# Router products inside the output projection, a float32 scatter, one more ring tile and a token-major last MLP

## The chip, the cores and the metric

The kernel runs on one core of a Trainium2 chip. The metric is the device time of one execution in microseconds (us). TensorE (PE) does the matrix products, and its weight loads (PEld) overlap them; VectorE (DVE) and ScalarE (ACT) do the elementwise work; GpSimd (POOL) is nearly idle; SyncE (SP) issues the DMA transfers that bring the weights from memory.

## The reference

Two blocks run one after the other on one sequence of 256 tokens of width 1024, each with two layers, all in float32.

```
def first_block(...):                       # two layers
        mod = c_act @ w_ada[layer] + b_ada[layer]        # 6 vectors: shifts, scales, gates
        h = rmsnorm(x, norm_mix_g[layer]) * (1.0 + sc_mix) + sh_mix
        mixed = token_mixer(h, ...)                      # SSD + HGRN + retention, then @ w_out
        x = x + g_mix * mixed
        h = rmsnorm(x, norm_ffn_g[layer]) * (1.0 + sc_ffn) + sh_ffn
        moe = hierarchical_moe(h, ...)                   # 32 experts in 4 groups, top 2, width 256
        x = x + g_ffn * moe
...
def second_block(...):                      # two layers, mixers RG-LRU and gated linear attention
        x = x + gt_m * rmsnorm_2(y, norm_g[i, 1])
        h = rmsnorm_2(x, norm_g[i, 2]) * (1.0 + sc_f) + sh_f
        y = conv_ffn(h, ...)                             # (gelu(conv(up)) * conv(up)) @ w_down
        x = x + gt_f * rmsnorm_2(y, norm_g[i, 3])
```

## The kernel before

**Layout.** Activations lie with channels on the partitions: `self.x` is 128 partitions x 8 channel groups x 256 tokens. A dense product is taken in three float32r matmuls (`mm3`, L517): both factors are split into a high part (rounded to float32r, `wh` by ACT in L509) and a rest (`wl` by DVE in L510), and the product of the two rests is dropped. Products that are written in plain float32 appear in the trace as two matmul instructions each.

**Weights.** Every weight comes as a tile of 1 MB by a DMA on SP's queue, in one fixed list (`make_plan`), into a ring of tiles (`Ring`): 8 tiles from the start, 3 more (`NM`) to the end of the mixture of experts, 6 more (`NX`) from the output projection on, and `NY` more from the start of the mixture of experts on. A transfer is issued when a tile of the ring comes free (`done`, `pump`), so SP stands still while the ring is full.

**The modulation vectors** (`ada`, tile `ad`, L299) are products of the conditioning vector with 96 weight tiles; four matmuls (eight instructions) a tile. Tables of numbers (`PRE`, `MIX`, `MOE`, `SP`, `FILL`) say how many of these tiles are taken up at which place in the list of weights and in TensorE's program.

**A layer of the first block.** After the token mixer, `out_proj` makes four projections `t` of 48 matmuls (tile `pj`), each for channel groups `2t` and `2t+1`; DVE adds each to `x`. `then(k)` makes the router's products for channel group `k`: two transposes (`htp`, L891), two products with the router's weights and two sums of squares (`rsum`, L893 and L896). They follow one projection later, and those of groups 6 and 7 at the end. Then come four `ad` tiles (`SP[7]`), while DVE works out the routing in a chain of small operations that ends in the one-hot matrix `oh`; `rkp` (L970) ranks the tokens of each expert.

**The mixture of experts** (`moe`) handles the 32 experts in eight blocks of four with 32 slots for each expert, and one further block `x` for a fully loaded expert, in the order 0 to 6, `x`, 7. For each block: `gp` (L1055) gathers the tokens of the slots, `gu` (L1095) makes gate and up products, `hdt` turns them, `dn` (L1136) makes the down product, and `scatter` (tile `ya`, L1153) adds the slots to the tokens through a matrix `P` of zeros and ones. For the scatter, the result `dn` is kept as a float32r high part `ys0` (a copy by ACT, L1140) and a rest `ys1` (a subtraction by DVE, L1141), and each of the eight channel groups takes two matmuls. Scatter of block `b` stands behind `gu` of block `b+2`. `overflow` (L1195) is a branch that would redo experts with more tokens than slots; here it is not taken.

**The second block.** Each of its two layers ends in `ffn`: 22 up products (`fup`, two projections of 128 channels each, with convolution and gelu) give `F`, and 22 x 8 x 3 = 528 matmuls (tile `fd`) multiply `w_down` (stationary) with `F` (256 tokens moving). After the last layer, `residual` scales and normalises the result and adds it to `x`, and four DMAs write `x` out.

## Time and profile before

| | |
|---|---|
| median of 3 runs | 1569.04 us (1565.69 to 1571.34) |
| the profiled execution | 1566.22 us, of which the span in the trace is 1564.1 us |
| granted TensorE clock, mean | 0.966 of full speed |
| busy: PE, DVE, ACT, POOL | 93%, 53%, 42%, 0% of the span |
| moved by DMA | 453.02 MB, 290 GB/s on average |

The share of busy time is an average over stages. In the two mixtures of experts (about 220 to 444 us and 645 to 870 us) the DMA engines are full; in the two MLPs of the second block TensorE is. What a piece of work costs is therefore to be read stage by stage, from what each stage waits for last.

### The profile page before, as it was taken

To read this page: it belongs to the slowest core of one execution; us is meant where nothing else is said; L and a number is where in the kernel's file an instruction comes from. 1 tells how busy PE (TensorE), PEld (TensorE's weight loads), DVE (VectorE), ACT (ScalarE), POOL (GpSimd) and SP (SyncE) were. 2 spreads that over 40 slices of the span, in tenths; PEclk is the share of its full clock that TensorE was granted. 3 is DMA by queue.
4 is the path that set the end of the run, shared out by engine and by line. 5 is a ranking of instruction groups with operands and counts; after the bars stand their busy time and mean duration, and the time that the engine had idled before them with its cause. 6 is when DMAs were issued, how large, how long until landed. Compare 5 with 4: busy or idle time off the path is not lost. (4 is left out here: it accounts for less than half of the span.)

```text
span 1564.1 us, 28414 instructions
## 1 busy us (share of the span) xinstructions
PE 1447.1 (93%) x11988; PEld 1143.9 (73%) x11988; DVE 824.1 (53%) x1580; ACT 656.1 (42%) x1098; POOL 3.0 (0%) x11
## 2 busy tenths in 40 slices
PE   4999999878989999897889999999999999899997
PEld 2868876434457778754445688799996997799996
DVE  3585631100157755311011667888846675788853
ACT  3534522111144254321121486566634544466643
POOL 0000000000000000000000000000000000000000
PEclk8999999989989999999899999999999999999999
DMA  9976789999998368899999877955546644655520
GB/s 379 420 278 243 277 326 421 421 421 420 416 393 348 121 243 329 333 420 420 421 420 415 335 291 283 375 190 186 176 159 245 244 162 157 221 193 185 189 82 28
DMA packets 64954, 453.02 MB, mean 290 GB/s; under 512 B 7088, under 2 KB 7728, under 8 KB 11440
## 3 DMA queue, kind: packets, MB, share of 16 engines
q1 hardware_dynamic: 63520, 446.94, 73.5%
q10 hardware_dynamic: 1296, 4.15, 0.7%
q8 instruction: 98, 1.61, 0.4%
q14 instruction: 40, 0.33, 0.1%
HBM read 450.01 MB, written 1.05 MB: 288 GB/s over the span
## 5 line engine op out<-in xcount | busy, mean ns | idle before, releaser
L517 PE MATMUL pj<-act,wh 128*128 128x256 f32 x3136 | 582.1, 287 | 20.3 <-ACT act L464 12.6
L517 PEld LDWEIGHTS pj<-act,wh 128*128 128x128 f32 x3136 | 494.8, 194 | 55.9 <-ACT act L464 15.3
L517 PE MATMUL pj<-act,wl 128*128 128x256 f32 x1568 | 446.2, 285 | 0.6 <-DVE wl L510 0.6
L510 DVE TENSOR_TENSOR wl<-wt,wh 128x1024 fp32r<-128x1024 f32 x260 | 317.2, 1223 | 222.7 <-ACT wh L509 220.0
L509 ACT ACTIVATE wh<-wt 128x1024 fp32r<-128x1024 f32 x260 | 274.3, 1059 | 345.8 <-PE pj L517 269.4
L517 PEld LDWEIGHTS pj<-act,wl 128*128 128x128 f32 x1568 | 303.3, 193 | 3.0 <-issue 1.2
L1095 PE MATMUL gu<-wt,xsl 128*32 128x256 f32 x2048 | 148.5, 410 | 36.8 <-DMA wt<-in_wu 33.8
L1095 PEld LDWEIGHTS gu<-wt,xsl 128*32 128x32 f32 x2048 | 72.4, 117 | 103.2 <-DMA wt<-in_wu 44.9
L517 PE MATMUL fd<-F,wh 128*128 128x256 f32 x704 | 125.0, 281 | 0.0
L1136 PE MATMUL dn<-wt,hT 128*32 128x512 f32 x528 | 114.5, 613 | 0.9 <-ACT hT L1116 0.9
L299 PE MATMUL ad<-wt,cz 128*32 128x512 f32 x768 | 112.9, 614 | 0.0
L517 PEld LDWEIGHTS fd<-F,wh 128*128 128x128 f32 x704 | 107.8, 188 | 0.2 <-ACT wh L509 0.2
L1104 DVE SCALAR_TENSOR_TENSOR sg<-sg,inf,gu 128x256 f32<-128x256 f32 x16 | 7.7, 480 | 180.6 <-ACT sg L1102 180.5
L517 PE MATMUL fd<-F,wl 128*128 128x256 f32 x352 | 98.6, 281 | 0.0
L1102 ACT ACTIVATE sg<-gu 128x256 f32<-128x256 f32 (+1 forms) x18 | 6.9, 382 | 212.5 <-PE gu L1095 206.1
L567 DVE SCALAR_TENSOR_TENSOR u<-pj,par,u 128x255 f32<-128x255 f32 (+1 forms) x176 | 84.3, 479 | 3.0
L1058 ACT ACTIVATE xsl<-gp,mod,gsm 128x128 f32<-128x128 f32 x128 | 48.1, 456 | 57.0 <-PE gp L1055 57.0
L1055 PEld LDWEIGHTS gp<-G,ht 128*128 128x128 f32 x512 | 62.2, 200 | 11.0 <-issue 11.0
L1055 PE MATMUL gp<-G,ht 128*128 128x128 f32 x512 | 65.7, 285 | 1.6 <-DVE G L1033 1.6
L517 PEld LDWEIGHTS fd<-F,wl 128*128 128x128 f32 x352 | 66.3, 188 | 0.0
L1136 PEld LDWEIGHTS dn<-wt,hT 128*32 128x32 f32 x528 | 26.4, 111 | 51.7 <-issue 43.2
L1153 PEld LDWEIGHTS ya<-P,ys 128*128 128x128 f32 (+1 forms) x288 | 36.9, 188 | 28.7 <-issue 12.8
(395 smaller groups left out, 1524.0 us busy)
## 6 DMA issues: line engine op xcount, KB each, us to landing
wt<-in_ada SPq DMA_DIRECT2D x96, 1024.0 KB, 6.9
wt<-in_wg SPq DMA_DIRECT2D x66, 1024.0 KB, 19.8
wt<-in_wu SPq DMA_DIRECT2D x66, 1024.0 KB, 19.8
wt<-in_wd SPq DMA_DIRECT2D x66, 1024.0 KB, 19.8
wt<-in_fup SPq DMA_DIRECT2D x44, 1024.0 KB, 4.9
wt<-in_win SPq DMA_DIRECT2D x26, 1024.0 KB, 12.9
wt<-in_fdn SPq DMA_DIRECT2D x22, 1024.0 KB, 4.8
wt<-in_glain SPq DMA_DIRECT2D x12, 1024.0 KB, 6.9
```

The lines of the kernel that those rows point to most:

```text
L299: nc.tensor.matmul(acc[32 * g:32 * g + 32], cz[:, k, :], w[:, 512 * g:512 * g + 512], start=k % 4 == 0, stop=k % 4 == 3, tile_position=(0, ...
L509: nc.scalar.activation(wh, raw, AF.Copy)
L510: nc.vector.tensor_tensor(wl, raw, wh, op=OP.subtract)
L517: nc.tensor.matmul(out, lhs[a], rhs[b], start=first and i == 0, stop=last and i == 2)
L567: nc.vector.scalar_tensor_tensor(out[:, d:], src[:, :T - d], w(taps - 1 - d), out[:, d:], op0=OP.mult, op1=OP.add)
L1055: nc.tensor.matmul(gp[:, kk], ht[:, k + kk, cc], G[:, cc].rearrange("p a b -> p (a b)"), start=kk == 0 and cc == 0, stop=kk == 3 and cc == 1)
L1058: nc.scalar.activation(xs[:, kk], gp[:, kk - k], AF.Identity, scale=self.gs[:, kk:kk + 1], bias=self.sh[:, kk:kk + 1])
L1095: nc.tensor.matmul(gu[q, m], xs[:, k, q], w[j][:, k], start=k == 0 and m == 0, stop=k == KD - 1 and m == 1, tile_position=(0, CAP * j))
L1102: nc.scalar.activation(sg[:n], gu[:n, 0], AF.Silu)
L1104: nc.vector.scalar_tensor_tensor(hid[:n], sg[:n], inf[:, 1:2], gu[:n, 1], op0=OP.mult, op1=OP.mult)
L1136: nc.tensor.matmul(dn[q], hT[b][:, j, q], w[n][i][:, 512 * j:512 * j + 512], start=j == 0, stop=j == 1, tile_position=(0, CAP * i))
L1153: nc.tensor.matmul(ya[k // 2][:, k % 2], ys[b][j][:m, k], Ps[b][:m], start=b == BLOCKS[0] and j == 0 and k % 2 == 0, stop=b == BLOCKS[-1] ...
```

## The change

- `out_proj` places the router products of the pair of channel groups before between the two halves of a projection, in place of behind it.
- The scatter takes `ys` and `P` in plain float32: one product for each channel group. ACT copies two of the four channel groups of each half of `dn`, DVE the other two.
- The ring has one tile more in the mixtures of experts (`NY` 2). The slots `xsl` have one buffer in place of two (`x4`), and the results `ys` are one tile in place of two.
- Two `ad` tiles move in the list of weights (`MIX`, `MOE`, `SP[7]`).
- An activation on `self.warm` stands in the text behind `turn(7, hid)`.
- The last MLP gives its result by token: `F` is stationary, and `w_down` moves with 512 columns. `turn_x` turns `x` (16 transposes) and spreads the gain over the partitions (8 float32 products) during the up products; `last` normalises and adds by token, and the output is written by token.
- `overflow` works on one half of the tokens at a time (left out below).

```diff
-NY = 1
+NY = 2
...
+    def proj(self, ps, key, hl, rows=False, first=False, between=None):
...
         for j in range(2):
             wp = self.take(key, j)
+            if j and between:
+                between()
...
     def out_proj(self, ps, key, hl, gate, then):
+        def pair(t):
+            for k in range(2 * t, 2 * t + 2):
+                then(k)
         for t in range(4):
-            acc = self.proj(ps, key + (t,), hl, first=t == 0)
+            acc = self.proj(ps, key + (t,), hl, first=t == 0, between=t and (lambda: pair(t - 1)))
...
-            for k in range(max(2 * t - 2, 0), 2 * t):
-                then(k)
-        for k in range(6, 8):
-            then(k)
+        pair(3)
...
-            P = sb.tile([128, T], R32, name="P", bufs=3)
+            P = sb.tile([128, T], F32, name="P", bufs=3)
...
-                ys[b] = [sb.tile([128, KD, 128], R32, name=f"ys{j}", bufs=1) for j in range(2)]
+                ys[b] = sb.tile([128, KD, 128], F32, name="ys", bufs=1)
...
-                nc.scalar.activation(y[0][:m, s], v, AF.Copy)
-                nc.vector.tensor_tensor(y[1][:m, s], v, y[0][:m, s], op=OP.subtract)
+                nc.scalar.activation(y[:m, s][:, :2], v[:, :2], AF.Copy)
+                nc.vector.tensor_copy(y[:m, s][:, 2:], v[:, 2:])
...
-                for j in range(2):
-                    nc.tensor.matmul(ya[k // 2][:, k % 2], ys[b][j][:m, k], Ps[b][:m],
-                                     start=b == BLOCKS[0] and j == 0 and k % 2 == 0,
-                                     stop=b == BLOCKS[-1] and j == 1 and k % 2 == 1)
+                nc.tensor.matmul(ya[k // 2][:, k % 2], ys[b][:m, k], Ps[b][:m], start=b == BLOCKS[0] and k % 2 == 0,
+                                 stop=b == BLOCKS[-1] and k % 2 == 1)
...
         turn(7, hid)
+        nc.scalar.activation(self.warm, self.eps, AF.Abs_reciprocal_sqrt, bias=self.eps, scale=0.0)
...
+    def turn_x(self, ps, sb, g, gate):
+        nc = self.nc
+        self.xt = sb.tile([128, 2, D], F32, name="xt", tag="z")
+        self.row = sb.tile([128, D], F32, name="ggrow")
+        gg = sb.tile([128, KD], F32, name="gsc", bufs=2)
+        nc.vector.tensor_tensor(gg, g, gate, op=OP.mult)
+        for h in range(2):
+            for cc in range(2):
+                tp = ps.tile([128, 512], F32, name="xtp", tag="ps")
+                for k in range(4):
+                    nc.tensor.transpose(tp[:, 128 * k:128 * k + 128], self.x[:, 4 * h + k, 128 * cc:128 * cc + 128],
+                                        self.c("ident"))
+                nc.scalar.activation(self.xt[:, cc, 512 * h:512 * h + 512], tp, AF.Copy)
+                yield
+            tp = ps.tile([128, 512], F32, name="ggp", tag="ps")
+            for k in range(4):
+                nc.tensor.matmul(tp[:, 128 * k:128 * k + 128],
+                                 gg[:, 4 * h + k:4 * h + k + 1].to_broadcast([128, 128]), self.c("ident"),
+                                 start=True, stop=True)
+            nc.scalar.activation(self.row[:, 512 * h:512 * h + 512], tp, AF.Copy)
+            yield
+    def last(self, ps, sb, acc, out):
+        nc, V = self.nc, self.nc.vector
+        for cc in range(2):
+            part = sb.tile([128, 2], F32, name="lsum", bufs=2)
+            for h in range(2):
+                sq = sb.tile([128, 512], F32, name="lsq", tag="k2")
+                nc.scalar.activation(sq, acc[cc][h], AF.Square, accum_out=part[:, h:h + 1])
+            s = sb.tile([128, 1], F32, name="lss", bufs=2)
+            V.tensor_tensor(s, part[:, 0:1], part[:, 1:2], op=OP.add)
+            r = self.rsqrt(sb, s, [128, 1], D, "")
+            for h in range(2):
+                w = slice(512 * h, 512 * h + 512)
+                t = sb.tile([128, 512], F32, name="lt", tag="k2")
+                V.scalar_tensor_tensor(t, acc[cc][h], r, self.row[:, w], op0=OP.mult, op1=OP.mult)
+                V.tensor_tensor(t, t, self.xt[:, cc, w], op=OP.add)
+                nc.sync.dma_start(out[cc, :, w], t)
...
+            if between and j > 3:
+                next(between, None)
...
+            if between:
+                for cc in range(2):
+                    s = slice(128 * cc, 128 * cc + 128)
+                    for h in range(2):
+                        for j, wp in zip(js, wps):
+                            self.mm3(acc[2 * cc + h].rearrange("p a b -> p (a b)"), [F[0][:, j, s], F[1][:, j, s]],
+                                     [w[:, 4 * h:4 * h + 4].rearrange("p a b -> p (a b)") for w in wp],
+                                     j == 0, j == NF - 1)
+                continue
...
-            es, sb = self.phase(f"moe{l}", there, k1=3, k2=2, x4=2, k8=1)
+            es, sb = self.phase(f"moe{l}", there, k1=3, k2=2, x4=1, k8=1)
...
-            update = self.residual(ps, sb, acc, prev[:, 3], gate, z(), norm=False)
-            for k in range(0, KD, 2):
-                update(k)
-                nc.sync.dma_start(out[:, k:k + 2], self.x[:, k:k + 2])
+            self.last(ps, sb, acc, out)
...
-MIX = ((4, 13, 2), (4, 13, 3), 11, 0, 4)
-MOE = (4, 4)
-SP = (0, 0, 0, 9, 15, 13, 13, 4, 0)
+MIX = ((4, 13, 0), (4, 13, 1), 11, 0, 4)
+MOE = (6, 6)
+SP = (0, 0, 0, 9, 15, 13, 13, 6, 0)
```

**On TensorE, at the end of `out_proj` of the first layer,** before the change: the last matmuls of projection 3 (`pj`), then the router products of groups 4 to 7 (three rows a group: `htp`, `rsum` with the router's weights `wrt`, `rsum` of the squares `rsq`), then the `ad` tiles (`cz` is the conditioning vector).

```order
L517 MATMUL pj<-act_1697,wh 128x256
L517 MATMUL pj<-act_1696,wl 128x256
L891 MATMUL htp<-cst_71,x 128x128 x2
L893 MATMUL rsum<-wrt,x 128x36 x2
L896 MATMUL rsum<-cst_71,rsq 128x1 x2
...
L896 MATMUL rsum<-cst_71,rsq 128x1 x2
L299 MATMUL ad<-wt_1475,cz_108 32x512 x4
```

The same place of the changed kernel, from the middle of projection 3 on:

```order
L894 MATMUL htp<-cst_71,x 128x128 x2
L896 MATMUL rsum<-wrt,x 128x36 x2
L899 MATMUL rsum<-cst_71,rsq 128x1 x2
L517 MATMUL pj<-act_1696,wh 128x256
...
L517 MATMUL pj<-act_1696,wl 128x256
L299 MATMUL ad<-wt_1475,cz_108 32x512
L894 MATMUL htp<-cst_71,x 128x128 x2
L896 MATMUL rsum<-wrt,x 128x36 x2
L899 MATMUL rsum<-cst_71,rsq 128x1 x2
...
L299 MATMUL ad<-wt_1475,cz_108 32x512 x3
```

Groups 4 and 5 now stand ahead of the second 24 matmuls of projection 3; behind it only one matmul of an `ad` tile stands ahead of groups 6 and 7, whose `x` needs that projection.

**On TensorE, at the end of the mixture of experts of the first layer,** before the change: the second half of block 7's down product (`dn`) and its scatter (`ya`, from the high part `ys_6269` and the rest `ys_6270`), then the next norm's first products.

```order
L1136 MATMUL dn<-wt_6122,hT 32x512
L1136 MATMUL dn<-wt_6124,hT 32x512 x2
L1153 MATMUL ya<-P,ys_6269 128x256 x2
L1153 MATMUL ya<-P,ys_6270 128x256
L1153 MATMUL ya<-P,ys_6269 128x256
L1153 MATMUL ya<-P,ys_6270 128x256 x2
L1153 MATMUL ya<-P,ys_6269 128x256
L1153 MATMUL ya<-P,ys_6270 128x256
L381 MATMUL nm<-nsq,cst_71 32x256 x2
```

The same place of the changed kernel, with the scatter of the first half:

```order
L1139 MATMUL dn<-wt_8563,hT 32x512
L1155 MATMUL ya<-P,ys 128x256 x4
L1139 MATMUL dn<-wt_8563,hT 32x512
...
L1139 MATMUL dn<-wt_8565,hT 32x512 x2
L1155 MATMUL ya<-P,ys 128x256 x4
L381 MATMUL nm<-nsq,cst_71 32x256 x2
```

Eight matmuls for each half have become four, of another type; nothing else has moved.

**On ScalarE, at the end of the kernel,** before the change: the last weight splits (`wh`), then scaled copies `z` and squares `nsq` of the result for the norm, with the load of a function table among them, and the reciprocal root `rs_y` at the end.

```order
L509 ACTIVATE wh<-wt_19269 128x1024 x2
L1264 ACTIVATE z<-fd,gsc 128x256 x2
L412 ACT_TABLE_LOAD
L412 ACTIVATE warm<-fd,eps 128x1
L416 ACTIVATE nsq<-fd 128x512
...
L358 ACTIVATE rs_y<-nm,eps 128x256
```

The same place of the changed kernel (`lsq` are squares, `lsum` and `lss` their sums by token):

```order
L509 ACTIVATE wh<-wt_24105 128x1024 x2
L1483 ACTIVATE lsq,lsum<-fd 128x512 x2
L358 ACT_TABLE_LOAD
L358 ACTIVATE rs_y<-lss,eps 128x1
L1483 ACTIVATE lsq,lsum<-fd 128x512 x2
L358 ACTIVATE rs_y<-lss,eps 128x1
```

The table load now stands behind the squares of the first 128 tokens, and the norm takes no matmul.

## Rows read from the trace of the kernel before

**Rows 1.** The page: engines' busy time, and the chain that ended last by line.
```profile
PE 1447.1 (93%) x11988; PEld 1143.9 (73%) x11988; DVE 824.1 (53%) x1580; ACT 656.1 (42%) x1098; POOL 3.0 (0%) x11
...
PE pj L517 26%; PE fd L517 8%; PE ad L299 2%; PE lv L599 1%; PE gu L1095 1%; PE dn L1136 1%; PE ga L517 1%; PE ya L1153 1%; DVE wl L510 1%; DVE x L1292 0%; DVE modt L1291 0%; PE nm L381 0%; ACT wh L509 0%; PE adt L311 0%; DVE rs_q L363 0%
```

**Rows 2.** Windows: busy time by engine, PE clock, DMA share, GB/s.
```profile
240.00:370.00 130.00, 115.31 (x1113) 64.60 (x1115) 17.84 (x63) 27.36 (x68) 0.00 (x0) 0.96 1.01 421
...
1360.00:1480.00 120.00, 120.00 (x994) 119.90 (x993) 102.34 (x170) 76.48 (x125) 0.00 (x0) 0.99 0.54 184
```

**Rows 3.** Waits of PE in the first mixture of experts, 230 to 444 us.
```profile
PE gu L1095 <- DMA wt<-in_wu: 17.1, 11, 1.9
PE ya L1153 <- PEq L1195: 3.4, 1, 3.4
```

**Rows 4.** Timeline of PE, last DMA wait of each mixture of experts.
```profile
379.02 5.03 PE L1095 MATMUL gu<-wt,xsl 128*32 128x256 f32 x57 [1.51 <-DMA wt<-in_wu]
...
803.83 5.95 PE L1095 MATMUL gu<-wt,xsl 128*32 128x256 f32 x57 [1.89 <-DMA wt<-in_wu]
```

**Rows 5.** Timeline of PE at the router, first layer.
```profile
208.96 0.38 PE L891 MATMUL htp<-cst,x 128*128 128x128 f32 x2
...
211.05 0.42 PE L891 MATMUL htp<-cst,x 128*128 128x128 f32 x2
...
213.25 3.64 PE L299 MATMUL ad<-wt,cz 128*32 128x512 f32 x32
218.71 0.38 PE L970 MATMUL rkp<-oh,cst 128*128 128x32 f32 x2 [1.82 <-DVE w L984]
```

**Rows 6.** Timeline of DVE at the router, first layer.
```profile
209.16 0.87 DVE L856 SCALAR_TENSOR_TENSOR x<-pj,mod,x 128x256 f32<-128x256 f32 x2 [7.06 <-PE pj L517]
```

**Rows 7.** Timeline of SP (DMA issues) at the start of the first mixture.
```profile
216.09 14.55 SPq L213 DMA_DIRECT2D wt<-in_wd  x4
230.74 3.41 SPq L213 DMA_DIRECT2D wt<-in_wg  x4
```

**Rows 8.** Windows at the end of either router: columns as above.
```profile
226.00:230.00 4.00, 4.00 (x75) 2.42 (x77) 0.00 (x0) 2.79 (x5) 0.00 (x0) 1.00 0.04 12
...
650.00:654.00 4.00, 4.00 (x71) 2.59 (x73) 0.00 (x0) 3.23 (x7) 0.00 (x0) 1.00 0.59 244
```

**Rows 9.** Groups of the last MLP's down product, 1487 to 1551 us.
```profile
L517 PE MATMUL fd<-F,wh 128*128 128x256 f32 x352 | 62.5, 281 | 0.0
```

**Rows 10.** Timeline of PE, float32 products of a norm.
```profile
1196.12 1.03 PE L384 MATMUL nm<-nsq,gsc 128*128 128x256 f32 x4
1196.98 1.03 PE L384 MATMUL nm<-npr,cst 128*128 128x256 f32 x4
```

**Rows 11.** Timeline, end of the first mixture of experts, all engines.
```profile
442.23 1.28 ACT L412 ACT_TABLE_LOAD   x1
442.24 0.69 DVE L1141 TENSOR_TENSOR ys<-dn,ys 128x512 fp32r<-128x512 f32 x1 [0.36 <-ACT ys L1140]
...
442.99 0.97 PE L1153 MATMUL ya<-P,ys 128*128 128x256 f32 x6 [0.22 <-DVE ys L1141]
...
444.00 1.67 ACT L416 ACTIVATE nsq<-x 128x512 f32<-128x512 f32 x3 [0.18 <-PE ya L1153]
```

**Rows 12.** Windows with a lowered PE clock: columns as above.
```profile
404.00:412.00 8.00, 7.21 (x26) 3.42 (x27) 0.00 (x0) 0.00 (x0) 0.00 (x0) 0.79 1.01 414
822.00:830.00 8.00, 8.00 (x35) 3.44 (x34) 1.54 (x3) 0.60 (x1) 0.00 (x0) 0.57 1.01 420
```

**Rows 13.** Timeline of PE: 128-column float32 products.
```profile
388.58 2.94 PE L1055 MATMUL gp<-G,ht 128*128 128x128 f32 x24
```

**Rows 14.** Timeline, end of the kernel, all engines.
```profile
1549.94 0.28 PE L517 MATMUL fd<-F,wl 128*128 128x256 f32 x1
...
1555.51 1.29 DVE L1291 TENSOR_TENSOR modt<-z,rs_y 128x512 f32<-128x512 f32 x2
...
1559.12 1.28 DVE L1292 TENSOR_TENSOR x<-x,modt 128x512 f32<-128x512 f32 x2
```

More of the change, by code (lines that the diff above doesn't have):

```diff
@@ L517, in mm3 @@
             nc.tensor.matmul(out, lhs[a], rhs[b], start=first and i == 0, stop=last and i == 2)
-    def proj(self, ps, key, hl, rows=False, first=False):
+    def proj(self, ps, key, hl, rows=False, first=False, between=None):
         nc = self.nc
@@ L1226, in overflow @@
-                nc.scalar.activation(hid, gu[0], AF.Silu)
-                nc.vector.tensor_tensor(hid, hid, gu[1], op=OP.mult)
-                nc.vector.tensor_tensor(hid, hid, wb.unsqueeze(1).to_broadcast([128, 2, T]), op=OP.mult)
-                for n in range(2):
-                    for j in range(2):
-                        o = 1024 * n + 512 * j
-                        v = part(self.A["wd"][l, e][:, o:o + 512]).rearrange("f (k p) -> f k p", k=4)
-                        for k in range(4):
-                            nc.tensor.matmul(ya[2 * n + k // 2][:, k % 2], v[:, k], hid[:, j], start=False, stop=False)
+                    t = slice(128 * cc, 128 * cc + 128)
@@ new lines, in overflow @@
+                    wb = ps.tile([128, 128], F32, name="wb", tag="ps")
+                    nc.tensor.matmul(wb, ov[:, cc, e:e + 1].to_broadcast([128, 128]), c("ident"), start=True, stop=True)
+                    gu = [ps.tile([128, 2, 128], F32, name="ogu", tag="ps") for _ in range(2)]
+                    for m, name in enumerate(("wg", "wu")):
+                        src = self.A[name][l, e].rearrange("(p k) f -> p (k f)", p=128)
+                        for k in range(KD):
+                            if k % 2 == 0:
+                                v = part(src[:, 256 * k:256 * k + 512]).rearrange("p (k j f) -> p k j f", k=2, j=2)
+                            for j in range(2):
+                                nc.tensor.matmul(gu[m][:, j], v[:, k % 2, j], h(k)[:, t], start=k == 0 and j == 0,
+                                                 stop=k == KD - 1 and j == 1)
@@ new lines, in overflow @@
+                    nc.scalar.activation(hid, gu[0], AF.Silu)
+                    nc.vector.tensor_tensor(hid, hid, gu[1], op=OP.mult)
+                    nc.vector.tensor_tensor(hid, hid, wb.unsqueeze(1).to_broadcast([128, 2, 128]), op=OP.mult)
+                    for n in range(2):
+                        for j in range(2):
+                            o = 1024 * n + 512 * j
+                            v = part(self.A["wd"][l, e][:, o:o + 512]).rearrange("f (k p) -> f k p", k=4)
+                            for k in range(4):
+                                nc.tensor.matmul(ya[2 * n + k // 2][:, k % 2, t], v[:, k], hid[:, j], start=False,
+                                                 stop=False)
@@ L1472, in ffn @@
                              j == 0 and o % 2 == 0, j == NF - 1 and o % 2 == 1)
+        if between:
+            acc = [a.rearrange("p a b -> p (a b)") for a in acc]
+            return [acc[:2], acc[2:]]
         return acc
@@ L1870 @@
            for n, a in arrays.items()}
-    out = nc.dram_tensor("out_0", (128, KD, T), F32, kind="ExternalOutput").ap()
+    out = nc.dram_tensor("out_0", (2, 128, D), F32, kind="ExternalOutput").ap()
     with tile.TileContext(nc) as tc:
```

20 lines of the change are left out of this document (5 added, 15 removed).

## The prediction

> **What bounds the kernel now.** I read the page first: TensorE is busy for 93% of the span, and the chain that ended last is nearly all its matmuls [rows 1]. That is an average over stages, so I then took windows by stage. In the mixture of experts the DMA engines are full, at 421 GB/s, from 240 us on, and TensorE waits; in the second block's MLP TensorE is busy for 120 of 120 us while the DMA share is 0.54 [rows 2]. So work on TensorE costs its full time in the MLP, and it may be free in the mixture of experts.
>
> How much of the mixture is ruled by the DMA is the question on which most of this change rests, so I looked at the waits. In the first one TensorE waits 17.1 us for weights, in 11 waits, and 3.4 us at the overflow branch [rows 3]. The last wait for a weight ends at 379.02 us, in block 6, and in the second layer at 803.83 us, also in block 6 [rows 4]. The scatter of block 7 ends near 444 us [rows 11]. So in the last 65 us of this stage TensorE is not waiting for any weight: it works through a backlog of blocks 6, `x` and 7. Each mixture therefore has two parts: up to block 6 the DMA stream sets the pace, and matmuls are covered by waits of about 5 us a block (17.1 us and some over four paced blocks); behind it TensorE sets the pace, and each matmul counts.
>
> **The change part by part.** All terms are made against the profiled execution (1566.2 us, span 1564.1); it lies 2.8 us below the median of 1569.0. I carry the difference over to the median.
>
> *Router products in the middle.* Before, projection 3 ends near 208.96 us. Groups 4 and 5 follow for 2.1 us, up to 211.05, and groups 6 and 7 for another 2.2 us, up to 213.25 [rows 5]. VectorE adds projection 3 to `x` from 209.16 on, 0.87 us for both groups, so done at 210.03 [rows 6]: groups 4 and 5 cover that wait. After, groups 4 and 5 lie inside the projection, which ends 2.1 us later. Behind it TensorE has one `ad` matmul, then waits for group 6. VectorE starts 0.2 us behind the last `pj` and takes 0.44 us for the group, and 0.25 us is my estimate, from such gaps in the timeline, for the handover: TensorE loses 0.9 us; groups 6 and 7 take 2.2. The router's sums are then complete 2.1 + 0.9 + 2.2 = 5.2 us behind the old end of the projection, where they took 4.3: **+0.9 us a layer**. Bounds: 0, if the `ad` matmul is all that is needed there, and +2, if the DVE chain meets its in-order `adrow` addition late. The `ad` tiles behind (3.64 us) and the chain of VectorE that `rkp` waits for [rows 5] move as a block. It is no gain either way: TensorE's work is the same, and its cover is smaller.
>
> *One more ring tile.* SP issues the last tile that fits at some time after 216.09, and stands until 230.74, when the first block's `gu` frees a tile [rows 7]. Between 226 and 230 us the DMA engines are at 0.04; in the second layer they are at 0.59 between 650 and 654 [rows 8]. A tile is 1.05 MB, at 421 GB/s 2.5 us [rows 2]. One more tile lies ready when the stream resumes, so the DMA-paced part ends 2.5 us earlier in the first layer; in the second the hole is 0.41 x 4 = 1.6 us in that window and somewhat more behind it, so 2.2. **-2.5 and -2.2 us**. The stream resumes at the time of the first `gu`, so the 0.9 us of the router come on top. Bounds 0 and -2.5.
>
> *Float32 scatter.* A float32r matmul of 256 columns takes 62.5 / 528 = 0.118 us [rows 9] (352 and 176 matmuls in the two groups, whose busy time overlaps). Plain float32 products of the same shape are not in the scatter yet, but the norm has them: four instructions in 0.86 us, start to start [rows 10], so 0.215 us an instruction and 0.43 us a product, which is two instructions. A scatter goes from 16 x 0.118 = 1.9 us to 8 x 0.43 = 3.4 us: +1.55 us. There are nine of them a layer. Those of blocks 0 to 4 stand in front of the last DMA wait and are covered by it. Those of blocks 5, 6 and `x` are not: 3 x 1.55 = **+4.7 us a layer**. For block 7, the eviction loses its serial step (VectorE's subtraction of 0.69 us now follows ScalarE's copy [rows 11]; two parallel copies of half the size end some 0.4 us sooner), against two halves of 0.8 us more TensorE work of which the last is behind the last `dn`: **+0.3 us**. If the cover of the first scatters were gone they would add five more, 7.8 us a layer; if that of 5, 6 and `x` is there after all, they cost nothing. I take the full 4.7, because no weight is waited for behind block 6.
>
> *Table load earlier.* Before, it runs from 442.23 to 443.51 us, and the norm's squares start at 444.00, released by the scatter [rows 11]. It was not on the path. The `warm` line has no input that ties it to the place where it stands in the text. The ring's list with two `ad` tiles moved, the single buffers of `xsl` (TensorE's own order keeps gather behind the products that read the old slots) and the branch not taken are costed at **0**; their cover is the same DMA backlog, and without it a late `ad` tile would cost its 0.9 us.
>
> *Clock.* TensorE's granted clock was 0.79 between 404 and 412 us, behind 3.4 us at the branch, and 0.57 between 822 and 830 us, among products with few columns, both in the TensorE-paced part [rows 12]; of its two levels that is the lower, 1.2 GHz, for part of the first stretch and most of the second. At half clock 8 us do 4.6 us of work, so 3.4 us could come back in the second layer and 1.7 us in the first, or another such stretch could arise. I take **-1** of this in all, with -5 and +3 as bounds.
>
> *Last MLP.* 264 matmuls of 512 columns stand in place of 528 of 256. No float32r matmul of 512 columns is in the trace over the full array. From below, the float32 instructions of [rows 10], in which 256 columns pass twice, take 0.215 us: 264 x 0.217 = 57.3 us, so -5.2 us. From above, twice the row, 0.237 us: 62.5, so 0. I take the lower end: a float32 instruction of 128 columns takes 2.94 / 24 = 0.1225 us [rows 13], and twice as many columns take not 0.245 but 0.215, so there is a fixed part that weighs less as columns grow. **-5.2 us**.
>
> The Trainium skill (TensorE: Matmul & The Clock Gate, Back-to-back issue gap) gives the gap between isolated matmuls as N/2.4 + 2.5 ns, so 109 ns for 256 columns and 216 ns for 512, and it adds that in a stream the weight loads set the pace too. By the formula alone the halving is worth 528 x 0.1092 - 264 x 0.2158 = 0.7 us; the row has 0.118 where the formula has 0.109, so the trace does not agree with it at 256 columns.
>
> *Turning x.* 16 transposes and 8 float32 products of 128 columns, in the stage where TensorE has no idle time. 16 instructions and another 16 at 0.1225 us: **+4.0 us**, up to 6 if each group also stalls for a free bank. ScalarE has 43 of 120 us free there, and VectorE 18 [rows 2], which cover its six copies.
>
> *The tail.* Before, the last `fd` starts at 1549.94 and is done near 1550.2; the four additions end at 1560.40, and the output's transfer ends the span at 1564.1: 13.9 us [rows 14]. After, the first 128 tokens are complete 3.9 us before the last matmul. Their table load is over 1.7 us before it, and their four passes of VectorE (0.64 us each [rows 14]) end 1.7 us behind it. Then sum, root and three small steps for the second 128 tokens take 1.1 us, their four passes 2.6 us, to 5.3 us behind the last matmul, and the transfer 3.7: 9.0 us. **-4.9 us**, bounds -3 and -6.
>
> Sum: first layer 0.9 - 2.5 + 4.7 + 0.3 = +3.4; second +3.7; clock -1; end -5.2 + 4.0 - 4.9 = -6.1. In all **0.0**, so 1569 on the median. What the end gives the scatters take.
>
> **The rivals.** *A: the scatter is covered.* If blocks 5, 6 and `x` have slack that the waits do not show, the mixtures give -1.3 and -1.0 and the end -6.1: with the clock's -1, 1559.6 us. With one of the three in the open, 1562.7. For it: the DMA engines are still full there, at 1.01 [rows 12]. Against it: no wait for a weight behind block 6 in either layer [rows 4].
>
> *B: slower, because 512 columns cost twice 256.* If the wide matmul takes 0.237 us, its -5.2 vanish: 1574.2. It decides from 0.235 us a matmul on, where the sum passes +4.7. For it: no such matmul was ever timed here. Against: the fixed part above. The formula of the Trainium skill page named above would come out there too, by another way.
>
> *C: the change does not do what it says.* `ad` work does not move on TensorE, and `warm` floats. Costed at nothing already; the time is that of the forecast.
>
> **How the numbers follow.** 0.3% is 4.7 us, about what a measurement of this kernel can tell from no change. Forecast with C, 0.54: within it. A with its halves, 0.28: faster. B, or a chain at the router that is late by more than 2 us with more half-clock stretches, 0.18: slower. The range goes from A's full form to B's: 1560 to 1574.5. The forecast alone is 1565 to 1573.
>
> **What would show it.** Right: `ya` of 0.43 us a product; last DMA waits some 1.5 us earlier; TensorE's work from there to the mixture's end longer by 4 to 5 us in each layer; `fd` near 57 us; 9 us from the last `fd` to the end; +4 us in the up products. Wrong: DMA waits behind block 6 (then A), `fd` at 62 us (B), or lowered clock where there was none, in the router above all.

## The result, and the profile after

The change made the kernel slower. Its median is 1586.62 us (1586.13 to 1591.82, four runs), that of the kernel before on the same chip 1567.37 us: the ratio is **1.0127, interval 1.0096 to 1.0157**, or 19.9 us. The profiled execution has a span of 1584.0 us, where it had 1564.1, also 19.9 us more, so that the trace can be followed stage by stage.

The page of the kernel after, to be laid beside [rows 1]: TensorE is busy for 28 us more, with 250 instructions fewer. In the chain's order of lines `ya` now stands ahead of `dn`, and a wait for a weight appears that was not among the first there.

```profile
PE 1475.3 (93%) x11738; PEld 1151.1 (73%) x11738; DVE 815.5 (51%) x1585; ACT 649.4 (41%) x1101; POOL 3.0 (0%) x11
...
PE pj L517 26%; PE fd L517 8%; PE ad L299 2%; PE lv L601 1%; PE gu L1098 1%; PE ya L1155 1%; DMA wt<-in_wd 1%; PE dn L1139 1%; PE ga L517 0%; DVE wl L510 0%; ACT wh L509 0%; PE adt L311 0%; DVE x L1295 0%; DVE xc L1378 0%; PE ogla L643 0%
```

First the places that the prediction named. The timeline of PE after, both layers of the first block (start, duration, operation; in brackets the idle time ahead of it and what ended it):

```profile
215.40 3.63 PE L299 MATMUL ad<-wt,cz 128*32 128x512 f32 x30
221.37 0.38 PE L973 MATMUL rkp<-oh,cst 128*128 128x32 f32 x2 [2.34 <-DVE w L987]
...
223.46 6.71 PE L1058 MATMUL gp<-G,ht 128*128 128x128 f32 x32 [0.82 <-DVE G L1036]
230.09 6.25 PE L1098 MATMUL gu<-wt,xsl 128*32 128x256 f32 x112
...
380.72 4.91 PE L1098 MATMUL gu<-wt,xsl 128*32 128x256 f32 x43 [1.92 <-DMA wt<-in_wu]
...
422.98 3.72 PE L1155 MATMUL ya<-P,ys 128*128 128x256 f32 x16
...
653.07 0.61 PE L973 MATMUL rkp<-oh,cst 128*128 128x32 f32 x2 [2.33 <-DVE w L987]
...
661.56 2.80 PE L1098 MATMUL gu<-wt,xsl 128*32 128x256 f32 x48
...
812.13 5.63 PE L1098 MATMUL gu<-wt,xsl 128*32 128x256 f32 x57 [1.53 <-DMA wt<-in_wu]
...
845.08 1.01 PE L1155 MATMUL ya<-P,ys 128*128 128x256 f32 x2 [6.62 <-issue]
846.02 9.42 PE L1098 MATMUL gu<-wt,xsx 128*32 128x256 f32 x32
```

The same view of the kernel before, for the places of it that [rows 3 to 5] do not show: the first `gu` of each mixture, and what stands behind the overflow branch in the second layer.

```profile
220.80 5.44 PE L1055 MATMUL gp<-G,ht 128*128 128x128 f32 x32 [0.82 <-DVE G L1033]
226.17 7.11 PE L1095 MATMUL gu<-wt,xsl 128*32 128x256 f32 x128
...
650.62 7.11 PE L1095 MATMUL gu<-wt,xsl 128*32 128x256 f32 x128
...
831.02 0.35 PE L1153 MATMUL ya<-P,ys 128*128 128x256 f32 x1 [0.59 <-PEq L1195]
832.45 7.07 PE L1095 MATMUL gu<-wt,xsx 128*32 128x256 f32 x32 [1.07 <-DVEq L1195]
```

`PEq` and `DVEq` are the sequencers of TensorE and VectorE, which take the instructions in order; L1195 is the overflow branch. The last wait for a weight in block 6 has moved little in the first layer (379.02 to 380.72 us) and by 8.3 us in the second. Behind block 6 one more weight is waited for, a tile of block 7's down product at 884.55 us in the second layer, for 0.20 us; its transfer is the `DMA wt<-in_wd` of the page. From the first `gu` to block 6's last wait TensorE now takes 150.6 us in either layer, where it took 152.9 and 153.2. The largest new thing is at 845.08 us: behind the branch that skips the overflow, TensorE stands for 6.62 us, where it stood for 0.59 and 1.07 before, and the 32 `gu` instructions on `xsx` behind it then take 9.42 us in place of 7.07. The waits of PE in the second mixture, 660 to 892 us, give the same (waited for: us in total, times, longest):

```profile
PE gu L1098 <- DMA wt<-in_wu: 12.0, 8, 1.9
PE ya L1155 <- issue: 6.6, 1, 6.6
```

Where a mixture ends is seen on ACT, in the squares of the next norm, timeline after:

```profile
452.17 1.67 ACT L416 ACTIVATE nsq<-x 128x512 f32<-128x512 f32 x3 [2.08 <-PE ya L1155]
...
892.82 2.19 ACT L416 ACTIVATE nsq<-x 128x512 f32<-128x512 f32 x4 [2.42 <-PE ya L1155]
```

They began at 444.00 us [rows 11] and, in the second layer, at 869.67. So +8.2 and then +23.1 us have gathered by there. From block 6's last weight wait to the norm, a stretch that is called the mixture's tail below, the first layer takes 71.5 us where it took 65.0 (+6.5), the second 80.7 where it took 65.8 (+14.9). The prediction had +5.0 for either. The windows of these stretches and of the first layer's router, after (columns as in [rows 2]):

```profile
215.40:230.09 14.69, 11.54 (x73) 8.66 (x72) 8.78 (x56) 5.78 (x12) 0.00 (x0) 0.77 1.01 424
...
382.30:452.20 69.90, 66.27 (x452) 35.35 (x444) 9.81 (x28) 9.70 (x25) 0.00 (x0) 0.92 1.01 418
813.70:893.30 79.60, 71.51 (x460) 37.77 (x452) 10.34 (x30) 10.14 (x25) 0.00 (x0) 0.85 0.83 332
```

and before:

```profile
213.25:226.17 12.92, 10.28 (x75) 7.41 (x75) 8.74 (x56) 5.77 (x12) 0.00 (x0) 0.87 0.98 405
...
380.50:444.00 63.50, 58.36 (x456) 30.96 (x445) 11.33 (x26) 11.36 (x24) 0.00 (x0) 0.96 1.02 417
805.40:870.00 64.60, 61.69 (x460) 32.78 (x452) 11.73 (x28) 11.69 (x25) 0.00 (x0) 0.92 1.02 417
```

The column to read is the granted clock: 0.87 became 0.77 at the router, 0.96 became 0.92, and 0.92 became 0.85. Length times what is missing to 1 is 2.5 and 5.6 us in the first tail, 5.2 and 11.9 in the second: 3 and 7 us more of full speed are missing, a part of it in stands (stretches in which TensorE idles), where it costs nothing.

The end of the kernel, timelines: the first `fd` before, then after, all engines:

```profile
1487.26 0.40 PE L517 MATMUL fd<-F,wh 128*128 128x256 f32 x2
```

```profile
1513.86 0.39 PE L517 MATMUL fd<-wh,F 128*128 128x512 f32 x1
...
1575.33 0.40 PE L517 MATMUL fd<-wh,F 128*128 128x512 f32 x1
...
1578.09 1.41 DVE L1490 SCALAR_TENSOR_TENSOR lt<-fd,rs_y,ggrow 128x512 f32<-128x512 f32 x2
1579.42 1.28 DVE L1491 TENSOR_TENSOR lt<-lt,xt 128x512 f32<-128x512 f32 x2
```

The 264 wide matmuls take 61.5 us from the first start to the last, 0.234 us each; the 528 took 62.7 (1487.26 to 1549.94). From the last one's start, 1575.33, to the span's end are 8.7 us, where they were 14.2 (1549.94 to 1564.1, [rows 14]).

### The profile page after: what moved, and what is told of

The parts are those of the page before. It is cut to its first block, busy times and chain, and to the rows that moved or that the text cites. A ratio compares the mean times of both kernels' runs of the same rounds, so it can differ in the third digit from the quotient of the medians.

```text
span 1584.0 us, 27918 instructions
## 1 busy us (share of the span) xinstructions
PE 1475.3 (93%) x11738; PEld 1151.1 (73%) x11738; DVE 815.5 (51%) x1585; ACT 649.4 (41%) x1101; POOL 3.0 (0%) x11
## 3 DMA queue, kind: packets, MB, share of 16 engines
q1 hardware_dynamic: 63520, 446.94, 71.5%
## 5 line engine op out<-in xcount | busy, mean ns | idle before, releaser
L1098 PE MATMUL gu<-wt,xsl 128*32 128x256 f32 x2048 | 144.8, 412 | 23.7 <-DMA wt<-in_wu 23.7
L1139 PE MATMUL dn<-wt,hT 128*32 128x512 f32 x528 | 118.0, 645 | 1.1 <-ACT hT L1119 0.9
L1155 PE MATMUL ya<-P,ys 128*128 128x256 f32 (+1 forms) x288 | 71.0, 391 | 9.4 <-issue 6.6
L1155 PEld LDWEIGHTS ya<-P,ys 128*128 128x128 f32 (+1 forms) x288 | 52.1, 189 | 33.1 <-issue 16.1
L1058 PEld LDWEIGHTS gp<-G,ht 128*128 128x128 f32 x512 | 65.1, 208 | 10.2 <-issue 10.2
L517 PE MATMUL fd<-F,wh 128*128 128x256 f32 x352 | 62.5, 281 | 0.0
L517 PE MATMUL fd<-wh,F 128*128 128x512 f32 x176 | 55.5, 395 | 0.0
## 6 DMA issues: line engine op xcount, KB each, us to landing
wt<-in_wd SPq DMA_DIRECT2D x66, 1024.0 KB, 19.8
```

The lines of the kernel that those rows point to most:

```text
L517: nc.tensor.matmul(out, lhs[a], rhs[b], start=first and i == 0, stop=last and i == 2)
L1058: nc.tensor.matmul(gp[:, kk], ht[:, k + kk, cc], G[:, cc].rearrange("p a b -> p (a b)"), start=kk == 0 and cc == 0, stop=kk == 3 and cc == 1)
L1098: nc.tensor.matmul(gu[q, m], xs[:, k, q], w[j][:, k], start=k == 0 and m == 0, stop=k == KD - 1 and m == 1, tile_position=(0, CAP * j))
L1139: nc.tensor.matmul(dn[q], hT[b][:, j, q], w[n][i][:, 512 * j:512 * j + 512], start=j == 0, stop=j == 1, tile_position=(0, CAP * i))
L1155: nc.tensor.matmul(ya[k // 2][:, k % 2], ys[b][:m, k], Ps[b][:m], start=b == BLOCKS[0] and k % 2 == 0, stop=b == BLOCKS[-1] and k % 2 == 1)
```

## The experiments

All ratios are to the kernel before, timed on the same chip, and each kernel is named by the first part of its label (e2, f3); a microsecond figure behind one is the ratio's distance from 1 times 1567. Two theories stood against each other: the float32 scatter costs more than predicted and is all of it, or a part that was costed at nothing is not free, the branch above all.

**One part at a time.** Kernels that hold one part of the change, or all but one.

The scatter alone, in the kernel before:

```
-            P = sb.tile([128, T], R32, name="P", bufs=3)
+            P = sb.tile([128, T], F32, name="P", bufs=3)
...
-                for j in range(2):
-                    nc.tensor.matmul(ya[k // 2][:, k % 2], ys[b][j][:m, k], Ps[b][:m], ...
+                nc.tensor.matmul(ya[k // 2][:, k % 2], ys[b][:m, k], Ps[b][:m], ...
```

> The kernel before with the float32 scatter alone (single result tile, two parallel copies). Theory sum: only the 3 scatters behind the last DMA wait and the last one cost, +4.7 to +5.0 us a layer, so +9 to +10 us, to about 1577. Rival clock: the longer scatters also bring TensorE to its lower clock in that part, as in the changed kernel (there 3.1 and 6.7 us more were lost to it), so +14 to +19 us, to 1582 to 1587. Rival covered: the work is hidden, within 3 us of the kernel before.

Measured: 1579.52 us, 1.0071 (1.0045 to 1.0098), **+11.1 us**. The mixtures' tails take 71.4 and 73.5 us, 6.4 and 7.7 more than before. Its windows, to be laid beside those of before above, show the work as predicted and a clock that is lower in both:

```profile
380.50:450.30 69.80, 65.14 (x452) 34.80 (x444) 9.72 (x27) 9.67 (x24) 0.00 (x0) 0.94 1.02 417
811.70:883.70 72.00, 70.11 (x460) 36.82 (x452) 9.83 (x28) 9.66 (x24) 0.00 (x0) 0.88 1.00 408
```

The ring tile undone, and with it the scatter:

```
-NY = 2
+NY = 1
```

> The changed kernel with NY back at 1 (18 tiles in the ring). Theory ring: the DMA-paced part ends 2.5 us later in each layer and all behind it follows, so +5 us, to about 1591, with the last DMA wait some 2.5 us later. Rival: one tile is worth nothing because the stream is only shifted; within 2 us of 1586.6.

> The changed kernel with NY 1 and the float32r scatter with high part and rest. To be held against the changed kernel with NY 1 (1590.9). Theory sum with clock: the float32 scatter costs 11 us there as it does in the kernel before, so about 1580. Rival sum alone: 9.5 us, 1581.4. Rival interaction: the lowered clock of the last part comes from the branch and the router, not from the scatter; less than 7 us, above 1584.

Measured: 1590.88 us, 1.0153 (1.0120 to 1.0187), with the tile undone; 1578.98, 1.0072 (1.0048 to 1.0097), with the old scatter as well. So the tile gives 4.1 us (1.0153 less 1.0127), and the scatter costs 12.7 in this company.

The router products put back behind the projection, and alone in the kernel before:

```
-            acc = self.proj(ps, key + (t,), hl, first=t == 0, between=t and (lambda: pair(t - 1)))
+            acc = self.proj(ps, key + (t,), hl, first=t == 0)
...
+            if t:
+                pair(t - 1)
```

> The changed kernel with the router products behind each projection, as before. Theory sum: 0.9 us a layer less to the router's sums and 0.5 us less for the late adrow addition, so -2 to -3 us, to about 1584. Rival clock: TensorE's lowered clock in the gather and the rank products behind the router (3.6 and 3.3 us lost against 1.8 and 1.6 before) hangs on the same idle time and goes too, so -5 to -7 us, to about 1580. Rival nothing: within 1 us of 1586.6.

> The kernel before with the router products in the middle of the projection alone. Theory from the traces: 0.9 us later sums and 1.7 to 2.0 us of late adrow addition and lowered clock behind them, in each layer, so +5 to +6 us, to about 1573. Rival sum alone, as predicted: +1.8 us, 1569. Rival nothing: 1567.

Measured: 1581.74 us, 1.0094 (1.0065 to 1.0124), without, 5.2 us under the kernel after; 1573.54, 1.0034 (1.0023 to 1.0045), alone: **+5.3 us**. The timeline and a window of PE, and the timeline of DVE, of the kernel with this part alone show where; the last line is DVE's in the kernel before:

```profile
214.15 3.63 PE L299 MATMUL ad<-wt,cz 128*32 128x512 f32 x30
220.12 0.38 PE L973 MATMUL rkp<-oh,cst 128*128 128x32 f32 x2 [2.34 <-DVE w L987]
...
222.22 6.68 PE L1058 MATMUL gp<-G,ht 128*128 128x128 f32 x32 [0.82 <-DVE G L1036]
228.83 3.44 PE L1098 MATMUL gu<-wt,xsl 128*32 128x256 f32 x60
```

```profile
214.15:228.83 14.68, 11.52 (x74) 8.63 (x73) 8.81 (x56) 5.78 (x12) 0.00 (x0) 0.77 0.99 387
```

```profile
217.84 0.69 DVE L306 TENSOR_TENSOR adrow<-adrow,ad 128x512 f32<-128x512 f32 x1 [0.46 <-PE ad L299]
```

```profile
217.51 0.66 DVE L306 TENSOR_TENSOR adrow<-adrow,ad 128x512 f32<-128x512 f32 x1
```

The `ad` products start 0.90 us late (214.15 for 213.25 [rows 5]), to the hundredth what was predicted. But then VectorE waits 0.46 us for them in its `adrow` addition, where it had not waited, and that addition stands in order within the router's chain; `rkp` waits 2.34 us where it waited 1.82; and the gather `gp` takes 6.68 us where it took 5.44, while the granted clock from `ad` to `gu` is 0.77 where it was 0.87: more of it runs at the lower level, 1.2 GHz. From `ad` to `gu` that is 14.68 us for 12.92, another 1.8 us.

The overflow's body by halves of the tokens, alone in the kernel before. The body is skipped with this input; it has 3153 instructions on TensorE and 131 on VectorE, where it had 1617 and 67:

```
             for e in range(NE):
-                wb = ps.tile([128, T], F32, name="wb", tag="ps")
                 for cc in range(2):
...
+                    t = slice(128 * cc, 128 * cc + 128)
+                    wb = ps.tile([128, 128], F32, name="wb", tag="ps")
```

> The kernel before with the overflow branch by token halves alone (a longer body, skipped here). Theory branch length: the second layer's stand at the branch grows from 1.7 us to 5 to 7 us, as in all three runs with that body, so +4 to +5 us, to about 1572, and the first layer's stays between 2 and 4 us. Rival: the stand of the second layer comes with the other changes (shorter evictions, another place in the stream), and this kernel stays within 1.5 us of the kernel before.

Measured: 1576.5 us, 1.0046 (1.0029 to 1.0063), **+7.2 us** for code that does not run. Its timeline of PE in the second layer has two stands behind the branch, 8.6 us together:

```profile
834.67 0.35 PE L1153 MATMUL ya<-P,ys 128*128 128x256 f32 x1 [3.21 <-PEq L1195]
840.42 1.91 PE L1095 MATMUL gu<-wt,xsx 128*32 128x256 f32 x4 [5.40 <-DMA wt<-in_wg]
```

The label of the second is not to be trusted: that weight was issued at 802.04 us, and the tiles of `wg` land 19.8 us behind their issue.

Not all of the cost is there. In this execution the second mixture's first `gu` is already 5.7 us late: the first `adt` (the modulation, turned) comes 1.45 us late, and the first mixture's tail takes 69.5 us for 65.0, with less stand at the branch (2.0 us for 3.4) but a lower clock in its second half. Windows of e5, then of the kernel before:

```profile
422.00:452.00 30.00, 27.85 (x243) 13.63 (x235) 7.92 (x15) 7.60 (x14) 0.52 (x1) 0.91 1.02 416
```

```profile
420.00:446.00 26.00, 23.85 (x228) 12.68 (x226) 7.23 (x14) 6.61 (x13) 0.52 (x1) 1.00 1.02 415
```

The last MLP by token alone, in the kernel before:

```
+                            self.mm3(acc[2 * cc + h].rearrange("p a b -> p (a b)"), [F[0][:, j, s], F[1][:, j, s]],
+                                     [w[:, 4 * h:4 * h + 4].rearrange("p a b -> p (a b)") for w in wp],
+                                     j == 0, j == NF - 1)
```

> The kernel before with the last MLP by token alone. From the changed kernel's trace: +4.5 us in the up products, -1.4 us in the down product (0.2335 us a matmul of 512 columns), -5 us in the tail, so -2 us, to about 1566. Rival as predicted: 0.217 us a matmul, so -6 us, to about 1562. Rival start: if this edit is what makes the first 30 us slower by 1.2 us (first turned modulation at 30.6 in place of 29.4 us), it is -1 us.

Measured: 1565.12 us, 0.9985 (0.9972 to 0.9998), **-2.4 us**.

The five parts add up to 5.3 + 11.1 + 7.2 - 4.1 - 2.4 = +17.1 us of the 19.9; with the sizes of e7 for the scatter and of the pair below for the body it is +21.7. What is left lies within the intervals. The two profiled executions, which also differ by 19.9 us, show where it gathers:

| place | kernel after late by, us |
|---|---|
| first `adt` | 1.2 |
| first layer: first `gu`, last weight wait of block 6, norm | 3.9, 1.7, 8.2 |
| second layer: the same | 10.9, 8.3, 23.1 |
| last MLP: first `fd`, last `fd` | 26.6, 25.4 |
| end | 19.9 |

The first tail's +6.5 is the scatter's (+6.4 in e2). The second tail's +14.9 is 7.2 more than the scatter's 7.7.

**What about the branch?** The kernel after with the old body and its two slot buffers (and the old scatter and ring) beside e7, which has the new body and one slot buffer; and bodies cut to one expert, in either kernel:

```
-            for e in range(NE):
+            for e in range(1):
```

> The changed kernel with NY 1, the float32r scatter, and the overflow body and two slot buffers of before: what is left of the change is the router products in the middle, the last MLP by token, the list's tables and the warm line. To be held against the same kernel with the new body (1579.0). Theory: the body costs as much here as in the kernel before, 5 to 9 us, so 1570 to 1574. Rival: it is a matter of the kernel before alone; within 2 us of 1579.

> The changed kernel with an overflow body for one expert in place of 32; the body is skipped here in either case, so only an input with an overfull expert would miss work. Theory branch: the 2.3 us and 6.6 us that TensorE stands idle at the overflow branch are the price of jumping over a long body (instructions that have to be fetched), so both fall below 1 us, and the kernel gains 7 to 9 us, to about 1578. Rival: the stall is a matter of where the weight stream stands and not of the body's length; the two waits stay between 2 and 7 us and the time stays within 2 us of 1586.6.

> The kernel before with an overflow body for one expert (skipped here; only an input with an overfull expert would miss work). Theory branch length: the stands at the branch of 3.4 and 1.7 us fall to 0.9 us each, as in the changed kernel with a short body, so -3 us, to about 1565. Rival: the time of the branch is covered by the scatter's inputs, and nothing changes: 1568.

Measured: e10 1569.74 us, 1.0007 (0.9996 to 1.0017), 10.2 us under e7; no run has the slot buffers by themselves. What e10 keeps of the change, the router products, the last MLP, the moved `ad` tiles and the `warm` line, comes to +1.1 us, where the first two alone give +5.3 and -2.4: the tiles and the line cost nothing that shows. e1 1578.83, 1.0063 (1.0038 to 1.0088), 10.0 us under the kernel after; the stands in the second layer are 0.5 and 0.3 us, and its second tail takes 73.3 us, where the kernel after takes 80.7 and e2 73.5. (The profiled execution of e1 is the slowest of its six, 1585.75 us, so its whole span shows no gain.) Then a miss: e8, the kernel before with one expert, has no stand over 0.4 us there either and was to gain, yet took 1572.23, 1.0032 (1.0017 to 1.0047), +5.0 us. In its profiled execution, the second slowest of ten, TensorE waits 1.44 us for an `ad` weight at the start, and the mean clock is 0.956 for 0.966; I found no cause.

So is it where the code lies, or how much there is? The same body in reverse order, with one expert fewer, one more, and twice as many, all in the kernel before:

```
+            for e in reversed(range(NE)):
...
+            for e in range(NE - 1):
...
+            for e in [*range(NE), 0]:
...
+            for e in [*range(NE), *range(NE)]:
```

> The kernel before with the experts of the overflow branch taken in reverse order: as many instructions, in the same places, other addresses; the body is skipped. Theory length: what the two edits of that body cost (+9.3 us for halves, +5 us for one expert) comes with a body of another length, so this one stays within 1.5 us of the kernel before, with the first turned modulation at 29.4 us. Rival: any edit there does it (then 1572 or more, and 30.8 us); the cause would be neither length nor work.

> The kernel before with 31 experts in the skipped overflow body (an input with an overfull last expert would miss work). Theory any other length: the first turned modulation comes at 30.6 to 31.0 us in place of 29.4, and the time is +4 to +9 us. Theory monotone length: within 1 us of the kernel before, 29.4 us, since the body is 3% shorter. The one-expert body was slower, not faster, which speaks for the former.

> The kernel before with a 33rd pass in the skipped overflow body (one expert twice, which would be wrong if it were taken). Theory any other length: 30.6 to 31.0 us for the first turned modulation, +4 to +9 us. Theory monotone length: within 1 us of the kernel before.

> The kernel before with every expert twice in the skipped body (it would be wrong if it were taken). Theory monotone length: more than the +9 us of the halves, and over 5 us of standing at the branch in both layers. Theory any other length: +4 to +9 us, as for the others. Rival chance: 29.4 us and no change, as for the reversed body.

Measured: 1567.34 us, 1.0000 (0.9985 to 1.0016); 1567.27, 0.9997 (0.9982 to 1.0012); 1566.20, 0.9995 (0.9982 to 1.0008); and 1575.63, 1.0050 (1.0033 to 1.0068) with 64. Order and one expert up or down do nothing; twice the body costs 7.8 us, as the halves do.

Last, on which engine. TensorE's share doubled alone (3153 instructions), and VectorE's alone (131):

```
+                            for z in range(2):
+                                nc.tensor.matmul(gu[m][:, j], v[:, k % 2, j], h(k), ...
```

```
+                for z in range(3):
+                    nc.vector.tensor_tensor(hid, hid, gu[1], op=OP.mult)
```

> The kernel before with every expert matmul of the skipped body twice (3153 instructions of TensorE in place of 1617, the other engines as before; wrong if it were taken). Theory VectorE: what TensorE waits for behind the branch is VectorE's late sequencer, so no 5.4 us stand and the time within 2 us of the kernel before. Theory TensorE: the jump over twice the code holds TensorE itself, 5 us or more, and +6 to +9 us.

> The kernel before with VectorE's part of the skipped body at 131 instructions in place of 67, as in the body by halves (wrong if it were taken). Theory VectorE: the second layer has the 5.4 us stand behind the branch, TensorE's clock falls there, and +6 to +9 us. Theory TensorE or another engine: within 2 us of the kernel before, and at most 1.2 us of waiting for VectorE there.

Measured: 1570.60 us, 1.0023 (1.0010 to 1.0037), with TensorE's, and 1574.89, 1.0056 (1.0034 to 1.0078), with VectorE's. The wait of PE behind the second layer's branch, first with TensorE's doubled, then VectorE's:

```profile
PE ya L1153 <- PEq L1195: 3.1, 1, 3.1
```

```profile
PE gu L1095 <- DVEq L1195: 6.5, 1, 6.5
```

The products behind that stand with TensorE's doubled, and the second layer's norm on ACT, before and with VectorE's doubled:

```profile
835.34 7.09 PE L1095 MATMUL gu<-wt,xsx 128*32 128x256 f32 x32
```

```profile
869.67 2.19 ACT L416 ACTIVATE nsq<-x 128x512 f32<-128x512 f32 x4 [0.18 <-PE ya L1153]
```

```profile
877.66 2.19 ACT L416 ACTIVATE nsq<-x 128x512 f32<-128x512 f32 x4 [0.18 <-PE ya L1153]
```

Sixty-four more skipped instructions on VectorE go with a stand of TensorE of 6.5 us where 1.07 was, and the products behind take 9.75 us for 7.07. Up to the branch this kernel follows the kernel before to 0.1 us (last weight wait at 803.85 us); its next norm starts at 877.66, 8.0 us later. In this kernel's first layer the same body costs nothing (norm at 444.01). TensorE's own share gives the smaller stand of e5, but g1's 3.6 us are not there: the products behind that stand take 7.09 us, as before, and its second tail 64.8 us for 65.8. They gather earlier, 1.4 us by the first `adt`, 2.0 in the first tail and 2.3 from there to the second layer's last weight wait.

**Can the last MLP be had cheaper?** With it alone TensorE still waits for an activation at the start of the last up products; waits of PE in e6, from 1350 to 1500 us:

```profile
PE pj L517 <- ACT act L464: 3.2, 1, 3.2
```

The products for the gain's rows depend on the modulation alone, so they could fill it:

```
+        if between:
+            next(between)
+            next(between)
         for j in range(NF):
```

> The kernel before with the last MLP by token, and with the eight gain products of turn_x ahead of the up products, where TensorE waits 3.15 us for its input. Theory: they cost nothing there, so 2 us less than the last MLP by token alone (1565.1), to about 1563, and the input that TensorE waits for is no later. Rival: ScalarE's two copies of the gain delay the input, and nothing is gained: 1565.

> The kernel before with the last MLP by token, the eight gain products ahead of the up products, and the small product on VectorE that they need ahead of the modulation. Theory: they now lie in the 3.15 us in which TensorE waits, and 2 us of the 4.5 us go, so 1563. Rival: the filled wait also keeps TensorE's clock up for the first up products, 1 us more, 1562. Rival: ScalarE's copies of the gain delay the modulation and nothing is won, 1565.

Measured: first a miss, 1570.38 us, 1.0020 (1.0008 to 1.0033): VectorE's small product `gsc`, on which they depend, stood behind the whole modulation in its queue. Its waits of PE there:

```profile
PE ggp L1458 <- DVE gsc L1454: 7.6, 1, 7.6
```

With that product ahead of the modulation, 1562.18 us, **0.9965 (0.9953 to 0.9977)**, which beats the kernel before by 5.5 us and the one after by 25; the waits in the same stretch:

```profile
PE ggp L1459 <- DVE gsc L1454: 0.7, 1, 0.7
PE pj L517 <- DVE wl L510: 0.6, 1, 0.6
```

## Why the prediction was wrong

| step | predicted | measured |
|---|---|---|
| router products in the middle, two layers | +1.8 | +5.3 |
| ring tile | -4.7 | -4.1 |
| float32 scatter | +10.0 | +11.1 |
| single buffers, table load, branch not taken | 0 | +7.2 to +10 (the branch) |
| clock | -1 | within the rows above |
| last MLP: products, turning, tail | -5.2 + 4.0 - 4.9 | -2.4 |
| sum | 0.0 | +17.1 of +19.9 |

**The step that failed** is the one that costed "the branch not taken" at 0, with the DMA backlog as its cover. Two things were wrong in it. The diff rewrites a body that does not run, and I counted what it computes, not how long it is: a skipped body that is twice as long on VectorE makes that engine late behind the branch (g2, and f3 and e5 in their manner). And block 6 with its branch stands behind the last weight wait, in the part that the prediction itself says TensorE paces: no backlog covers it there. [rows 3] already showed 3.4 us of stand at this branch; that row should have been priced with both its layers. In the kernel after it costs 7.2 us of the second tail. That the body makes this stand is shown there by e1: with a short body the stand is gone, and the tail takes 73.3 us. That the wait is VectorE's is shown for g2 alone; the row of the kernel after says only `issue`, and which share TensorE's own longer body has in it is not shown.

**Router in the middle: mechanism right, size off.** The +0.9 to the `ad` products came. The bound said that more would come if VectorE "meets its in-order `adrow` addition late"; it does, by half a microsecond, and the gather behind it loses another 1.3 to the lower clock. So it was above the upper bound of +2: in e11 the first layer's `gu` starts 2.7 us late, and its second layer adds about as much again.

**Scatter: right.** The eight products of a scatter take 3.72 us, the pipeline's end included, for 3.4 predicted; behind block 6 no weight is waited for in e2, and for 0.20 us in the kernel after, so rival A fell. What e2 has on top of 5.0 us a layer, 1.4 and 2.7, goes with the clock (0.94 for 0.96 and 0.88 for 0.92).

**Ring tile: right**, 2.2 and 2.6 us earlier from the first `gu` to the last weight wait, for 2.5 and 2.2.

**Clock: wrong sign.** It was to give 1 us back; on balance it took more. Behind the 6.62 us the `xsx` products cost 2.3 us more than before, and behind the router's half microsecond `gp` costs 1.3 more. Not each stand does this: the `xsx` products take 7.09 us behind 3.15 us of stand in g1's second layer, and 7.09 behind 2.30 in the first layer of the kernel after, where they took 8.78 behind the 3.40 of [rows 3].

**Last MLP: one term mis-sized.** The wide matmul takes 0.234 us, near the upper end of 0.237 and not the lower of 0.217, so the down product got shorter by 1.2 us and not by 5.2 (the prediction's product uses 0.217, its row gives 0.215): nearly rival B's size, though the kernel became slower in other places than B's. The inference from a 128-column float32 instruction to a fixed part of a float32r one did not hold; a column costs 0.46 ns at 256 and at 512. The formula of the Trainium skill (TensorE: Matmul & The Clock Gate, Back-to-back issue gap) was nearer, with 0.7 us for the halving: its 109 and 216 ns stand in nearly the same ratio as the 118 and 234 of the rows, which are some 8% longer. Turning `x` came out (from the last `adt` to the first `fd` 137.3 us for 132.6, +4.6 for +4.0), and so did the tail (8.7 us from the last start for 14.2, -5.5, for -4.9).

**Open.** Why the longer body costs a stand of 5 us or more in the second layer and never in the first; why the first tail is 4.4 us longer in e5 and f3 (69.5 and 69.4 us) and not in g2, e7 and the kernel after; why g1's first layer is slower; why TensorE waits for an `ad` weight at the start in the kernel after (1.43 us) and in several of the others, so that the first `adt` comes at 30.6 us and not at 29.4 (+1.2 us of the 19.9); and e8.

## What to carry to other kernels

A branch that is not taken is not free, and its price can hang on the body's length: twice the body, or of VectorE's share of it, cost 7 to 9 us here, one expert more or fewer nothing, and one expert alone gave 10 us in one kernel and cost 5 in the other. So time a rewrite of rare code, and look at the waits behind the branch when it makes the body longer. When a change opens a stand on TensorE, even of half a microsecond, allow for what the products behind it will cost if they run at the lower clock level: 1.3 and 2.3 us here, though not behind each stand. And a shape that was never timed should be priced by its columns until a row says otherwise: halving the number of instructions by doubling their width gave 1.2 us in 63.

## What the hardware showed that was not expected

- Skipped code: 65 to 69 VectorE instructions in the body leave 1 to 1.7 us of stand in the second layer (3.15 where TensorE's share is doubled), 131 leave 5 to 9: twice the count, three times the stand and more. The first layer has 1 to 3.5 us with either.
- A float32r matmul of 128x512 takes 0.234 us from start to start at 2.4 GHz (granted clock 1.00), twice that of 128x256 (0.118).
- A small operation late in VectorE's queue held TensorE for 7.6 us (e12); the same operation one step earlier held it for 0.7 (f4).
